# Conv-FFN with h normed into a second buffer, and adaLN sections moved from TensorE to VectorE

## The chip, the cores and the metric

The kernel runs on one core of one Trainium2 chip. The metric is the time of one execution on the device, in microseconds; the median of several runs is given.

## The reference, cut to what matters

Four layers over 384 tokens (128 context tokens, 256 latent tokens) of width 1024, all in fp32. Layer i uses mixer i mod 3 (gMLP, pooling, attention), so layers 0 and 3 are gMLP. Each mixer and each FFN has a pre-norm with its own scale and shift (adaLN), which differ for the two groups of tokens:

```
sh1, sc1, gt1, sh2, sc2, gt2 = split(silu(cond) @ w_ada[i] + b_ada[i], 6)
h = rms_norm(x, g_mix[i]) * (1 + sc1) + sh1
x = x + gt1 * mixer(h)
h = rms_norm(x, g_ffn[i]) * (1 + sc2) + sh2
x = x + gt2 * conv_ffn(h)

def conv_ffn(h, w_in, conv_w, conv_b, w_out):          # D_FF = 2816
    a, u = split(h @ w_in, 2)
    a = ap[:-2] * conv_w[0] + ap[1:-1] * conv_w[1] + ap[2:] * conv_w[2] + conv_b
    return (gelu(a) * u) @ w_out
```

## The kernel before

Activations lie transposed: features on the 128 partitions (KD = 8 tiles), tokens along the row. A product in fp32 accuracy is three fp32r matmuls: each weight chunk is split into whi (ScalarE, line 338) and wlo (VectorE, line 345), each activation into a high and a low part (hh, hl; gh, gl), and `mm3` (line 638) issues hi x hi, lo x hi, hi x lo.

Weights come as chunks of 128 x 1024 through one SP queue into a ring of five raw buffers (`load`, `free`); split chunks have four buffers. `w_get` takes the next chunk and has the three after it split; the split of a chunk waits until TensorE has finished the chunk four before it. The order of the instructions on every engine is that of the program. The chunks of w_ada for later layers are woven into the same list of chunks by the table `ADA` ("ad": line 380, two products with a running sum on VectorE per section of 128 rows; "ap": line 398, four matmuls per section on TensorE, 8 records in the profile). `EDGES` says how many weight chunks of a stage go by before its first section and after its last.

Before each FFN, `prep` (line 582 to 588) writes hh, hl = the two parts of x times A, not yet normed, and puts the shift into two more columns: rows of TE = 386 columns. So the input matmuls can start before the sum of squares is complete. `ffn` (line 641) runs f = 0 and 1 together (chunks "fr"), takes the sums of squares (`stats`, line 521) at k = stat_k, builds a diagonal R from the reciprocal roots, spreads it with a matmul over all partitions and copies it to rbs (line 697). Then f = 2 to 21 follow, two chunks and 48 matmuls each. The epilogue of a tile (`epi_a`, `epi_b`, `epi_c`) multiplies a and u with rbs on VectorE (lines 657, 661), adds the shift's column (be, line 671), does the convolution (lines 673 on ScalarE, 675 on VectorE), Gelu (681), gg = (u + bu) * gelu in two instructions (684, one per group of tokens; bu is read from PSUM), and splits gg into gh and gl. f's epilogue stands in the stage of f + 1; those of 0 and 1 both in f = 2. Matmul outputs have six PSUM banks in turn: four for f = 0 and 1, two for each later f. Then `out_proj` multiplies gh, gl with w_out; its residuals feed the next `prep`.

Of the kernel before, what the change touches and what calls it, by code (L numbers as in the profile page):

```python
# [34 lines left out]
TE = T + 2  # L35
BUFS = 5
# [21 lines left out]
EDGES = {(0, "gv"): (2, 1), (0, "go"): (5, 0), (3, "gv"): (5, 2), "fi": (0, 6), (3, "go"): (5, 2)}  # L58
# [212 lines left out]
class Prog:  # L271
    def __init__(self, ctx, tc, a):
# [5 lines left out]
        self.wsp = pool("wsp", 4)  # L278
        self.tmp = pool("tmp", 2)
# [235 lines left out]
    def stats(self, *parts):  # L515
# [1065 lines left out]
```

## Time and profile before

| | |
|---|---|
| median of 3 runs | 1789.53 us (1789.23 to 1791.93) |
| profiled execution | 1789.65 us, span of its instructions 1787.8 us |
| busy in the span | TensorE 1766.3 us (matmuls overlap), VectorE 1387.9, ScalarE 873.9 |
| adaLN sections | 136 on VectorE (272 products), 40 on TensorE (320 records) |

The span runs from the first to the last instruction of the program; the execution's own time has a little more around it. Busy time of TensorE is modelled, since matmuls are pipelined: the distance from matmul to matmul says more. A releaser ("<-") is the engine whose event ended a wait.

### The profile page before, as it was taken

The numbers are of one execution on the slowest core, as the hardware profiler recorded it, in microseconds if no ns is written. First come the engines' busy times: TensorE is split into PE (matmuls) and PEld (weight loads), VectorE is DVE, ScalarE is ACT, GpSimd is POOL, SyncE is SP. The second block draws the span as 40 slices with busy tenths as digits, with TensorE's granted clock in tenths as the row PEclk, the third lists the DMA queues.
The fourth block names the chain that finished last, engine by engine and source line by source line (L and its number), as shares of the span: only waits on it lengthen the run. The fifth ranks groups of instructions, "written<-read, shape, count | busy, mean of one in ns | idle before, by whom it ended". The sixth has DMA issues, their size and how long they took to land.

```text
span 1787.8 us, 26990 instructions
## 1 busy us (share of the span) xinstructions
PE 1766.3 (99%) x10326; PEld 1682.8 (94%) x10326; DVE 1387.9 (78%) x2456; ACT 873.9 (49%) x1556; POOL 1.8 (0%) x30
## 2 busy tenths in 40 slices
PE   7999999999999999999999999999999999999999
PEld 5799899999998999999778999999988999999999
DVE  5877689998876888797787788878775787888732
ACT  3634335555445555432568465553354443555531
POOL 0000000000000000000000000000000000000000
PEclk9999999999999999999999999999999999999999
DMA  9775565554653444466543444436645255444341
GB/s 328 283 238 179 211 218 176 177 176 168 208 201 122 146 163 175 148 234 228 177 148 131 139 156 159 165 118 214 204 170 196 96 175 177 142 153 143 123 150 57
DMA packets 87637, 311.65 MB, mean 174 GB/s; under 512 B 10450, under 2 KB 10962, under 8 KB 87252
## 3 DMA queue, kind: packets, MB, share of 16 engines
q1 hardware_dynamic: 87364, 309.92, 49.8%
q8 instruction: 81, 1.33, 0.3%
q14 instruction: 48, 0.39, 0.1%
q10 hardware_dynamic: 144, 0.01, 0.0%
HBM read 308.06 MB, written 1.84 MB: 173 GB/s over the span
## 4 chain that ended last, share of the span: by engine, by line
PE 84%; DVE 10%; ACT 3%; issue 2%; DMA 1%; SPq 0%; DVEq 0%; ACTq 0%
PE mm L638 65%; PE mm L762 6%; DVE junk L380 3%; DVE wlo L345 2%; ACT whi L338 1%; PE S L638 1%; PE mm L806 1%; DMA wraw<-wts 1%; DVE ct L675 1%; PE S L1035 1%; PE psa L398 1%; PE adaT L638 1%; PE mm L928 1%; PE psa L762 1%; PE adaT L762 1%
## 5 line engine op out<-in xcount | busy, mean ns | idle before, releaser
L345 DVE TENSOR_TENSOR wlo<-wraw,whi 128x1024 fp32r<-128x1024 f32 (+2 forms) x390 | 465.8, 1200 | 188.7 <-ACT whi L338 187.7
L338 ACT ACTIVATE whi<-wraw 128x1024 fp32r<-128x1024 f32 (+2 forms) x390 | 399.7, 1035 | 305.3 <-PE mm L638 189.1
L638 PE MATMUL mm<-hh,whi 128*128 128x386 f32 (+1 forms) x1664 | 426.6, 341 | 0.0
L638 PE MATMUL mm<-hh,wlo 128*128 128x386 f32 (+1 forms) x1664 | 423.9, 340 | 0.7 <-DVE wlo L345 0.2
L638 PE MATMUL mm<-hl,whi 128*128 128x386 f32 (+1 forms) x1664 | 421.3, 338 | 0.0
L380 DVE SCALAR_TENSOR_TENSOR junk<-wraw,condb 128x1024 bf16<-128x1024 f32 x272 | 332.2, 1221 | 7.6 <-ACT condb L1499 2.7
L638 PEld LDWEIGHTS mm<-hh,whi 128*128 128x128 f32 x1664 | 300.6, 188 | 4.8 <-issue 2.1
L638 PEld LDWEIGHTS mm<-hh,wlo 128*128 128x128 f32 x1664 | 303.1, 188 | 2.0 <-DVE wlo L345 1.9
L638 PEld LDWEIGHTS mm<-hl,whi 128*128 128x128 f32 x1664 | 303.3, 188 | 0.0
L638 PE MATMUL mm<-gh,wlo 128*128 128x384 f32 x704 | 193.6, 336 | 0.0
L638 PE MATMUL mm<-gl,whi 128*128 128x384 f32 x704 | 193.6, 336 | 0.0
L638 PE MATMUL mm<-gh,whi 128*128 128x384 f32 x704 | 193.6, 336 | 0.0
L681 ACT ACTIVATE ct<-ct 128x385 f32<-128x385 f32 x88 | 46.1, 527 | 178.2 <-DVE ct L675 178.1
L638 PEld LDWEIGHTS mm<-gl,whi 128*128 128x128 f32 x704 | 128.5, 188 | 0.0
L638 PEld LDWEIGHTS mm<-gh,wlo 128*128 128x128 f32 x704 | 128.5, 188 | 0.0
L638 PEld LDWEIGHTS mm<-gh,whi 128*128 128x128 f32 x704 | 128.4, 188 | 0.0
L675 DVE SCALAR_TENSOR_TENSOR ct<-ab,par,ct 128x385 f32<-128x385 f32 x176 | 109.1, 621 | 22.3 <-ACT ct L673 17.4
L684 DVE SCALAR_TENSOR_TENSOR gg<-u,mm,ct 128x128 f32<-128x128 f32 (+1 forms) x176 | 66.3, 419 | 49.1 <-ACT ct L681 49.1
L586 ACT ACTIVATE hh<-x,A 128x128 fp32r<-128x128 f32 x96 | 43.2, 457 | 104.9 <-DVE x L453 94.1
L671 ACT ACTIVATE ab<-a,be 128x128 f32<-128x128 f32 (+1 forms) x176 | 70.7, 450 | 2.6
L657 DVE TENSOR_TENSOR a<-mm,rbs 128x384 f32<-128x384 f32 x88 | 48.6, 552 | 20.5 <-PE mm L638 14.5
L673 ACT ACTIVATE ct<-ab,par 128x385 f32<-128x385 f32 x88 | 62.7, 712 | 3.4
(301 smaller groups left out, 1961.9 us busy)
## 6 DMA issues: line engine op xcount, KB each, us to landing
wraw<-wts SPq DMA_DIRECT2D x562, 512.0 KB, 3.3
wraw<-wts SPq DMA_DIRECT2D x12, 256.0 KB, 2.6
wraw<-wts SPq DMA_DIRECT2D x8, 384.0 KB, 4.1
x<-x SPq DMA_DIRECT2D x4, 384.0 KB, 4.3
mx<-mix SPq DMA_DIRECT2D x1, 1280.0 KB, 7.1
y<-x SPq DMA_DIRECT2D x3, 384.0 KB, 3.1
condb<-condb SPq DMA_DIRECT2D x1, 1024.0 KB, 8.6
ws<-a_w_s SPq DMA_DIRECT2D x2, 512.0 KB, 4.0
```

The lines of the kernel that those rows point to most:

```text
L338: nc.scalar.activation(hi[:, :n], t[:, :n], AF.Copy)
L345: nc.vector.tensor_tensor(out=lo[:, :n], in0=t[:, :n], in1=hi[:, :n].bitcast(F32), op=ALU.subtract)
L380: nc.vector.scalar_tensor_tensor(out=self.junk.bitcast(BF16), in0=w, scalar=1.0, in1=self.condb[:, c, :], op0=ALU.mult, op1=ALU.mult, accu ...
L586: nc.scalar.activation(self.hh[:, d, t0:t1], self.x[:, d, t0:t1], AF.Copy, scale=A[:, d, c:c + 1])
L638: nc.tensor.matmul(o, w[:, c:c + nw], r, start=(first and p == 0), stop=(last and p == 2))
L657: nc.vector.tensor_tensor(out=a1, in0=pa[:, 0:T], in1=rbs, op=ALU.mult)
L671: nc.scalar.activation(ab[:, p0:p1], a1[:, t0:t1], AF.Identity, bias=be[:, c:c + 1])
L673: nc.scalar.activation(t, ab[:, 1:T + 2], AF.Identity, scale=cw[1], bias=cb)
L675: nc.vector.scalar_tensor_tensor(out=t, in0=ab[:, i:i + T + 1], scalar=cw[i], in1=t, op0=ALU.mult, op1=ALU.add)
L681: nc.scalar.activation(t, t, GELU)
L684: nc.vector.scalar_tensor_tensor(out=g[:, t0:t1], in0=u1[:, t0:t1], scalar=bu[:, c:c + 1], in1=t[:, t0 + c:t1 + c], op0=ALU.add, op1=ALU.mult)
L762: nc.tensor.matmul(ps[n][i], hs, w[p == 1][:, c:c + 512], start=(k == 0 and p == 0), stop=(k == 7 and p == 2))
```

## The change

There are two buffers hb[0] and hb[1] where hh and hl were one. For f = 0, 1 and 2 (NR = 3) an FFN works as before. Meanwhile `put_act` norms x again with rbs into the other buffer, with shift, in plain rows of 384: one multiply on VectorE, two affine activations and a copy on ScalarE, one subtract on VectorE for each of the eight k. From f = 3 on the matmuls read this buffer and 384 columns, and the epilogue has no multiply with rbs, copies a from PSUM, and has Gelu in two parts and one product. The epilogue of f = 0 stands in f = 2, that of 1 in f = 3, and so on; in f = 8 two are done, from then on the distance is one tile again. stat_k is 3 in place of 5 (layer 1: 6 in place of 7), and the spread comes two k after the sums, where the stage has that many left. The products of f = 14 to 21 are stored over the first buffer, which is no longer read. The gMLP's second half, the attention's qS and layer 3's u products use the buffers in the same way. 24 sections move from "ap" to "ad", (0,3), (0,4) and others change stage, and an FFN's sections lie between its 8th and its 40th chunk.

```
 ADA = {
-    (0, "gv"): [("ad", 0, 2)],
-    (0, "gu"): [("ad", 0, 3), ("ap", 0, 4)],
-    (0, "go"): [("ad", 0, 5), ("ap", 1, 1)],
-    (0, "fi"): [("ad", 1, 2), ("ad", 1, 0), ("ad", 1, 4, 0, 3)],
-    (0, "fo"): [("ad", 1, 4, 3, 8), ("ad", 1, 3)],
-    (1, "fi"): [("ad", 1, 5), ("ad", 2, 1, 0, 5)],
-    (1, "fo"): [("ad", 2, 1, 5, 8), ("ad", 2, 0), ("ad", 2, 4)],
-    (2, "nm"): [("ap", 2, 3, 0, 6)],
-    (2, "qkv"): [("ap", 2, 3, 6, 8)],
-    (2, "at"): [("ap", 2, 2), ("ap", 2, 5)],
-    (2, "fi"): [("ad", 3, 1), ("ad", 3, 2, 0, 3)],
-    (2, "fo"): [("ad", 3, 0), ("ad", 3, 2, 3, 8)],
-    (3, "gv"): [("ad", 3, 4), ("ad", 3, 3, 0, 1)],
-    (3, "go"): [("ad", 3, 3, 1, 8)],
+    (0, "gv"): [("ad", 0, 4)],
+    (0, "gu"): [("ad", 0, 2), ("ad", 0, 3, 0, 2)],
+    (0, "go"): [("ad", 0, 3, 2, 8), ("ad", 0, 5, 0, 3)],
+    (0, "fi"): [("ad", 0, 5, 3, 8), ("ad", 1, 1), ("ad", 1, 2), ("ad", 1, 0, 0, 5)],
+    (0, "fo"): [("ad", 1, 0, 5, 8), ("ad", 1, 4), ("ad", 1, 3)],
+    (1, "fi"): [("ad", 1, 5), ("ad", 2, 1), ("ad", 2, 0)],
+    (1, "fo"): [("ad", 2, 4), ("ad", 2, 3)],
+    (2, "nm"): [("ap", 2, 2, 0, 6)],
+    (2, "qkv"): [("ap", 2, 2, 6, 8)],
+    (2, "at"): [("ap", 2, 5)],
+    (2, "fi"): [("ad", 3, 1), ("ad", 3, 2)],
+    (2, "fo"): [("ad", 3, 0), ("ad", 3, 4, 0, 4)],
+    (3, "gv"): [("ad", 3, 4, 4, 8), ("ad", 3, 3, 0, 4)],
+    (3, "go"): [("ad", 3, 3, 4, 8)],
     (3, "fi"): [("ad", 3, 5)],
 }
-EDGES = {(0, "gv"): (2, 1), (0, "go"): (5, 0), (3, "gv"): (5, 2), "fi": (0, 6), (3, "go"): (5, 2)}
+EDGES = {(0, "gv"): (2, 1), (0, "go"): (5, 0), (3, "gv"): (5, 2), "fi": (8, 4), (3, "go"): (5, 2)}
...
+    def put_act(self, k, A, rbs, hi, lo, sh):
+        nc = self.nc
+        t = self.tmp.tile([128, T], F32, tag="sq", name="nt")
+        nc.vector.tensor_tensor(out=t, in0=self.x[:, k, :], in1=rbs, op=ALU.mult)
+        for c, (t0, t1) in enumerate(GRPS):
+            nc.scalar.activation(t[:, t0:t1], t[:, t0:t1], AF.Identity, scale=A[:, k, c:c + 1], bias=sh[:, k, c:c + 1])
+        nc.scalar.activation(hi[:, k, :], t, AF.Copy)
+        return lambda: nc.vector.tensor_tensor(out=lo[:, k, :], in0=t, in1=hi[:, k, :].bitcast(F32), op=ALU.subtract)
...
+    def plain(self, n):
+        w, o = KD * T, PLAIN[n]
+        return [self.hb[n][:, w * i + o:w * i + w + o].rearrange("p (k t) -> p k t", t=T) for i in range(2)]
...
     def ffn(self, l, pr, follow, stat_k):
...
+        nh, nl = self.plain(1 - self.cur)
+        tail = self.plain(self.cur)
...
+            gh, gl = ([own[i][:, f, :] if f < NG else tail[i][:, f - NG, :] for f in range(NF)] for i in range(2))
...
             def epi_a(f, pa, pu):
+                if f >= NR:
+                    return f, pa, None, pu, None
...
-                    nc.scalar.activation(ab[:, p0:p1], a1[:, t0:t1], AF.Identity, bias=be[:, c:c + 1])
+                    if f < NR:
+                        nc.scalar.activation(ab[:, p0:p1], a1[:, t0:t1], AF.Identity, bias=be[:, c:c + 1])
+                    else:
+                        nc.scalar.activation(ab[:, p0:p1], a1[:, t0:t1], AF.Copy)
...
+                if f >= NR:
+                    for c, (t0, t1) in enumerate(GRPS):
+                        nc.scalar.activation(g[:, t0:t1], t[:, t0 + c:t1 + c], GELU)
+                    nc.vector.tensor_tensor(out=g, in0=u, in1=g, op=ALU.mult)
+                    return g
...
+            def norm(n):
+                ks, to_norm[:] = to_norm[:n], to_norm[n:]
+                for i in range(0, len(ks), 2):
+                    for lo in [self.put_act(k, pr["A"], rbs, nh, nl, sh) for k in ks[i:i + 2]]:
+                        lo()
...
                     if k == stat_k:
                         R = self.diag(self.stats(pr["acc"], pr["sq"]))
+                    if k == stat_k + 2:
+                        nc.scalar.activation(rbs, self.spread(R), AF.Copy)
+                        R = None
                     self.mm3([(b[i], 512 * k2 + 128 * i) for i in range(4)], w, (hh[:, k, :], hl[:, k, :]),
                              k == 0, k == 7)
-            nc.scalar.activation(rbs, self.spread(R), AF.Copy)
+                    if k > stat_k + 1:
+                        norm(2)
+            if R is not None:
+                nc.scalar.activation(rbs, self.spread(R), AF.Copy)
+            norm(2)
             prev = [(0, b[0], b[1]), (1, b[2], b[3])]
             for f in range(2, NF):
-                pa, pu = self.bank()[:, :TE], self.bank()[:, :TE]
+                w0 = TE if f < NR else T
+                pa, pu = self.bank()[:, :w0], self.bank()[:, :w0]
+                now, prev = (prev, []) if f == 8 else (prev[:1], prev[1:])
...
+                    if f < NR:
+                        norm(3)
                     for k4 in range(4):
                         k = 4 * kk + k4
-                        self.mm3([(pa, 256 * k4), (pu, 256 * k4 + 128)], w, (hh[:, k, :], hl[:, k, :]), k == 0, k == 7)
-                prev = [(f, pa, pu)]
+                        r = (hh[:, k, :], hl[:, k, :]) if f < NR else (nh[:, k, :], nl[:, k, :])
+                        self.mm3([(pa, 256 * k4), (pu, 256 * k4 + 128)], w, r, k == 0, k == 7)
+                prev.append((f, pa, pu))
...
-            pr = self.ffn(l, pr, follow, 7 if kind == 1 else 5)
+            pr = self.ffn(l, pr, follow, 6 if kind == 1 else 3)
```

## Rows read from the trace of the kernel before

**Rows 1.** The page's busy list: busy us, share, instructions.

```profile
PE 1766.3 (99%) x10326; PEld 1682.8 (94%) x10326; DVE 1387.9 (78%) x2456; ACT 873.9 (49%) x1556; POOL 1.8 (0%) x30
```

**Rows 2.** The chain that ended last, shares by line, whole span.

```profile
by line: PE mm L638 65.2%; PE mm L762 6.4%; DVE junk L380 3.0%; DVE wlo L345 2.4%; issue 1.9%; ACT whi L338 1.4%; PE S L638 1.4%; PE mm L806 1.2%; DMA wraw<-wts 1.2%; DVE ct L675 1.1%; PE S L1035 1.0%; PE psa L398 0.7%; PE adaT L638 0.7%; P
```

**Rows 3.** Stretches: us, then busy of PE, PEld, DVE, ACT, POOL; clock; DMA.

```profile
272.00:443.50 171.50, 170.83 (x960) 169.43 (x960) 154.17 (x251) 92.72 (x165) 0.00 (x0) 1.00 0.50 173
443.50:536.00 92.50, 92.50 (x538) 92.50 (x537) 76.52 (x130) 43.24 (x71) 0.00 (x0) 1.00 0.59 201
584.00:753.70 169.70, 169.70 (x961) 169.70 (x960) 146.22 (x235) 95.08 (x168) 0.00 (x0) 1.00 0.45 159
```

**Rows 4.** Waits of TensorE and its weight loads, 60 us to the end: total, times, longest.

```profile
PE Tps L421 <- ACT T L1244: 1.0, 1, 1.0
...
PEld mm L638 <- DVE wlo L345: 1.9, 4, 0.5
```

**Rows 5.** Matmuls in two stretches (xcount), and a piece of the chain.

```profile
600.00:740.00 140.00, 140.00 (x793) 1.00 0.47 166
770.00:830.00 60.00, 60.00 (x348) 1.00 0.77 261
...
163.23 8.44 PE mm L638 x48
```

**Rows 6.** Groups by line: busy us and mean ns; line 398.

```profile
L398 PE MATMUL psa<-wraw,cond 128*32 128x256 f32 x320 | 24.3, 389 | 0.8 <-DMA wraw<-wts 0.8
```

**Rows 7.** Pieces of the chain, layers 1 and 2: start, us, what.

```profile
583.97 261.38 PE mm L638 x1488
...
1009.19 10.59 PE mm L638 x60
1019.78 1.23 PE cs L521 x12
...
1028.12 265.57 PE mm L638 x1512
```

**Rows 8.** Timeline of VectorE, layer 2: start, us, what.

```profile
1022.28 0.56 DVE L530 TENSOR_TENSOR R<-ident,rs 128x384 f32<-128x384 f32 x1
```

**Rows 9.** Timeline of ScalarE, layer 2.

```profile
1028.16 0.49 ACT L697 ACTIVATE rbs<-adaT 128x384 f32<-128x384 f32 x1 [3.77 <-PE adaT L536]
...
1030.27 0.79 ACT L671 ACTIVATE ab<-a,be 128x128 f32<-128x128 f32 x2
...
1033.38 1.28 ACT L681 ACT_TABLE_LOAD   x1
```

**Rows 10.** Timeline of VectorE, layer 0, one tile f.

```profile
394.19 1.22 DVE L380 SCALAR_TENSOR_TENSOR junk<-wraw,condb 128x1024 bf16<-128x1024 f32 x1
...
396.60 1.27 DVE L675 SCALAR_TENSOR_TENSOR ct<-ab,par,ct 128x385 f32<-128x385 f32 x2
398.46 0.76 DVE L684 SCALAR_TENSOR_TENSOR gg<-u,mm,ct 128x128 f32<-128x128 f32 x2 [0.59 <-ACT ct L681]
399.41 1.23 DVE L345 TENSOR_TENSOR wlo<-wraw,whi 128x1024 fp32r<-128x1024 f32 x1 [0.19 <-ACT whi L338]
400.56 0.55 DVE L568 TENSOR_TENSOR gl<-gg,gh 128x384 fp32r<-128x384 f32 x1
401.02 0.55 DVE L657 TENSOR_TENSOR a<-mm,rbs 128x384 f32<-128x384 f32 x1
...
401.96 1.21 DVE L345 TENSOR_TENSOR wlo<-wraw,whi 128x1024 fp32r<-128x1024 f32 x1
403.09 1.22 DVE L380 SCALAR_TENSOR_TENSOR junk<-wraw,condb 128x1024 bf16<-128x1024 f32 x1
```

**Rows 11.** Timeline of ScalarE, layer 0, the same tile.

```profile
397.91 0.53 ACT L681 ACTIVATE ct<-ct 128x385 f32<-128x385 f32 x1 [3.44 <-DVE ct L675]
398.34 1.04 ACT L338 ACTIVATE whi<-wraw 128x1024 fp32r<-128x1024 f32 x1
399.29 0.51 ACT L567 ACTIVATE gh<-gg 128x384 fp32r<-128x384 f32 x1
```

More of the change, by code (lines that the diff above doesn't have):

```diff
@@ L475, in sqrt_table @@
         nc = self.nc
-        d = self.tmp.tile([128, 1], F32, tag="dmy", name="dmy")
+        d = self.tmp.tile([128, 1], F32, tag="dmy", name="dmy", bufs=1)
         nc.scalar.activation(d, self.ones[:, 0:1], AF.Sqrt)
@@ L628, in prep_squares, with use @@
         return res, after
+    def use(self, n):
+        self.cur = n
+        w = KD * TE
+        self.hh, self.hl = (self.hb[n][:, w * i:w * i + w].rearrange("p (k t) -> p k t", t=TE) for i in range(2))
+    def plain(self, n):
+        w, o = KD * T, PLAIN[n]
+        return [self.hb[n][:, w * i + o:w * i + w + o].rearrange("p (k t) -> p k t", t=T) for i in range(2)]
     def mm3(self, outs, whl, rhl, first, last, nw=128):
@@ L703, in ffn @@
                         sts = []
-                        w = self.w_get("fi", mid=lambda: sts.extend([epi_a(*p) for p in prev]))
+                        w = self.w_get("fi", mid=lambda: sts.extend([epi_a(*p) for p in now]))
                         ts = [epi_b(st) for st in sts]
@@ L745, in gmlp @@
         nc = self.nc
-        hh, hl = self.hh[:, :, 0:T], self.hl[:, :, 0:T]
-        te = T if pr is None else TE
+        hb = self.cur if pr is None else 1 - self.cur
+        vh, vl = self.plain(hb)
+        tail = self.plain(1 - hb)
         with self.tc.tile_pool(name=f"gmlp{l}", bufs=1) as gp:
             v = gp.tile([128, 3, DG], F32, tag="v", name="v")
-            ga = gp.tile([128, 16, T], F32R, tag="ga", name="ga")
-            gb = gp.tile([128, 16, T], F32R, tag="gb", name="gb")
+            own = [gp.tile([128, 8, T], F32R, tag=n, name=n) for n in ("ga", "gb")]
+            ga, gb = ([own[i][:, c, :] if c < 8 else tail[i][:, c - 8, :] for c in range(16)] for i in range(2))
             ws = gp.tile([128, 8, 128], F32, tag="ws", name="ws")
@@ L869, in gmlp @@
             for m in range(m0, 8):
-                b = [self.bank()[:, :te] for _ in range(2)]
+                b = [self.bank()[:, :T] for _ in range(2)]
                 for kk in range(2):
@@ L1268, in store_lo @@
                                         op=ALU.subtract)
-            nc.scalar.activation(self.tmp.tile([128, 1], F32, tag="dmy", name="dmy"), self.ones[:, 0:1], AF.Exp)
+            nc.scalar.activation(self.tmp.tile([128, 1], F32, tag="dmy", name="dmy", bufs=1), self.ones[:, 0:1], AF.Exp)
             put(2)
@@ L1390, in attention @@
             store_lo(NP - 2)
-            self.out_proj("o", oh[:, :, 0, :], oh[:, :, 1, :], 8, l, 2, after, banks, drain, 0)
+            self.out_proj("o", [oh[:, s, 0, :] for s in range(NP)], [oh[:, s, 1, :] for s in range(NP)], 8, l, 2, after,
+                          banks, drain, 0)
             ex.close()
@@ L1400, in run @@
         self.x = self.const.tile([128, KD, T], F32, name="x")
-        self.hh = self.const.tile([128, KD, TE], F32R, name="hh")
-        self.hl = self.const.tile([128, KD, TE], F32R, name="hl")
-        self.par = self.const.tile([128, NPAR], F32, name="par")
+        self.hb = [self.const.tile([128, 2 * KD * TE], F32R, name=f"hb{i}") for i in range(2)]
+        self.use(0)
+        self.par = self.const2.tile([128, NPAR], F32, name="par")
         self.cst = self.const.tile([128, NCST], F32, name="cst")
@@ L1461, in a0_put @@
         def a0_put(d, A):
-            self.put([d], lambda k: A, rbs, self.hh[:, :, 0:T], self.hl[:, :, 0:T], 0)
+            self.put([d], lambda k: A, rbs, *self.plain(0), 0)
         nc.scalar.activation(self.cond[:, :, 0:2], cin, AF.Silu)
```

55 lines of the change are left out of this document (33 added, 22 removed).

## The prediction

> **What bounds the kernel now.** I read the page's busy list first, then the chain that ended last, then stretches of single stages, then timelines. TensorE is busy 99% of the span [rows 1], but matmuls are pipelined, so this says little; the chain says more: most of it is matmuls, 65% line 638 alone, with VectorE's adaLN products (junk), weight splits (wlo) and convolution (ct) as the next links [rows 2]. The stretches show where VectorE is near the limit: 154.17 of 171.50 us in the input stage of layer 0's FFN, 146.22 of 169.70 in layer 1's, 76.52 of 92.50 in layer 0's output stage, all at clock 1.00 [rows 3]. After the first 60 us TensorE hardly waits: the longest single wait of a matmul is 1.0 us, and VectorE's weight splits hold back the weight loads of line 638 four times, 1.9 us together [rows 4]. So the kernel is bound by matmul time, with VectorE close behind in layers 0 and 1. What takes matmul time away is worth its time; what makes VectorE or ScalarE later shows soon.
>
> **What is taken from TensorE.** (1) Columns. Tiles f = 3 to 21 of each FFN read 384 columns instead of 386: 19 tiles x 48 matmuls x 4 layers = 3648. Less the two records that straddle a stretch's edges, 140 us hold 791 matmuls of 386 columns, 177.0 ns each, and 60 us hold 346 of 384, 173.4 ns [rows 5]. 3648 x 3.6 ns = 13.1 us. Layer 3's gMLP changes 288 in the same way: 1.0 us. Layer 0's gMLP has 384 columns already, in rows of 386: 48 matmuls in 8.44 us, 175.8 ns [rows 5]. So most of the 3.6 ns goes with the rows' place, not with two columns; stored 384 apart, 384 x 2.4 ns = 0.9 us more. The bound below: if the new rows lie no better, only the 1.2 ns of the two columns, 4.7 us in place of 15.0.
> The Trainium skill (TensorE: Matmul & The Clock Gate, section "Back-to-back issue gap") gives an isolated warm matmul N/2.4 ns plus a fixed 2.5. Two columns would be 0.83 ns by that, 3936 matmuls 3.3 us, and the sum below some 11 us worse; the rows are longer than its figure at both widths and differ by more.
> (2) 24 adaLN sections leave TensorE. A section is 8 matmul records, 320 for 40 sections, 24.3 us [rows 6], 0.61 us each. The 16 in layer 0 stand in a stage that TensorE sets: 9.8 us. Layer 2's eight fill an attention stage with gaps. The chain holds 0.7% of 1787.8, 12.5 us, of psa [rows 2]; less the 9.8, 2.7 us are left for 24 attention sections, so eight give 0.9 (bounds 0 and 4.9).
> (3) The 1.9 us of waits in layer 0's FFN [rows 4] go, if VectorE is no longer late; it will be, below, and the new sum replaces them.
> Together 13.1 + 1.0 + 0.9 + 9.8 + 0.9 + 1.9 = 27.6 us.
>
> **What is put on the way: the norm before f = 3.** Layer 2 as the model, by its own clock. The input stage starts at 1009.19; 60 matmuls (five k) take 10.59, 2.12 per k; the twelve sums of squares take 1.23; f = 2 starts at 1028.12 [rows 7]. In the change the sums come at k = 3 and end at 1016.8. R was ready 1.8 us after their end (1022.84 against 1021.01) [rows 7, 8], so the spread at k = 5, at 1021.0, has it. Before, the spread followed three k after 1021.0, at 1027.4, and the copy rbs started at 1028.16 and took 0.49 [rows 9]: it ends 1.2 us after the spread begins, now at 1022.2. TensorE has three k and f = 2 left, so f = 3 is due at 1036.5 as before (1028.12 + 8.47).
> f = 3 takes the banks of f = 0: there are six, four for f = 0 and 1, two for f = 2. They are free only after f = 0's product gg, which reads its bias from the bank. All eight norms now stand before that epilogue in the order of both ScalarE and VectorE. One pair: VectorE multiply 0.55 (as gl) [rows 10]; ScalarE two affine parts 0.79 (as ab) [rows 9], 0.1 to the dependent copy, copy 0.51 [rows 11], the second k 1.31 later; VectorE subtract. With 0.03 per hand-over that is 0.55 + 0.03 + 2.72 + 0.03 + 0.46 = 3.8 us, and the next pair can't start sooner, since VectorE's subtract of the second k stands ahead of it. Four pairs 15.2, plus 1.6 for a weight split between the first two: norms end at 1039.0. Then f = 0: multiply 0.55, be 0.2, ab 0.8 and 0.1, ct 0.71 (1041.4), VectorE's two ct 1.28, in the shadow of which the table load of 1.28 runs [rows 9], Gelu 0.55, gg 0.76: 1044.1. **f = 3 waits 7.6 us**, in layers 0, 2 and 3. Bound below: ScalarE alone, without any wait (8 x 1.31, two splits, the epilogue, table load, Gelu, gg), ends at 1039.4: 2.9 us. I take the chain, for the two engines hand over twice in every pair.
> Queued behind this wait are all later matmuls, and ScalarE's splits of the chunks whose buffers they free; VectorE and ScalarE catch up meanwhile. In layers 0 and 2 the first adaLN section (after the split of chunk 9) comes ahead of f = 1's epilogue, now one tile later than before: 0.6 us at f = 4 in layer 2.
> Layer 1 spreads after the stage. f = 2 starts at 583.97 [rows 7], rbs ends at 584.5, one pair to 588.3; f = 0's multiplies and a weight split 2.1, ct 1.6; then three more norms (3.8 + 2.5) before its Gelu: table load 1.28, Gelu, gg, 600.4 against 592.4 due: 8.0. Three norms, a split and an adaLN section (2.41) then stand before f = 1's gg, 615.7 against 608.8: 6.9 more.
> Sum: 3 x 7.6 + 0.6 + 14.9 = 38.3 us; bound below 3 x 2.9 + 4.4 = 13.1.
>
> **VectorE per tile, with more adaLN.** In layer 0 VectorE sets the pace already: 403.09 - 394.19 = 8.90 us per tile with one section [rows 10], against 48 x 177.0 = 8.50 of TensorE. A section is 396.60 - 394.19 = 2.41. The new epilogue drops a and u (0.93) and halves gg to one instruction (0.46). But VectorE's wait for Gelu stays, since nothing stands between ct and gg, and Gelu is two activations now, 0.8 as ab instead of 0.53. The next weight split waits for whi, which starts 0.1 before Gelu's end and takes 1.04 [rows 11]: from ct's end to wlo's start were 1.54 us (397.87 to 399.41), with gg inside; 0.27 for the longer Gelu makes it 1.80. Per tile: ct 1.27 + 1.80 + wlo 1.15 + gl 0.46 + wlo 1.13 = 5.81, plus 2.41 per section. The sections of a stage now lie in 32 of its 44 chunks, 16 tiles: layer 0 has 26 (1.625 per tile), 9.73 us; layer 1 24 (1.5), 9.43; layer 2 16, 8.22; layer 3 8, 7.02; against 48 x 173.4 = 8.32 of TensorE. Layers 2 and 3 fit. Layer 0 loses 1.41 x 16 = 22.6, layer 1 1.11 x 16 = 17.8, less the lead that VectorE can lose first: before, 18 tiles of 0.40 too much are 7.2 us, of which TensorE felt 1.9, so 5.3. **17.3 and 12.5 us.** Bound below: with before's idle of 0.78 per tile (0.59 and 0.19, [rows 10]) in place of 1.34, 0.85 and 0.55 too much, 8.3 and 3.5.
> Layer 0's output stage takes six more sections, 76.52 + 6 x 2.5 = 91.5 of 92.50 us [rows 3]: bounds 0 and 5, I take 1. Its other stages have room.
>
> **Costed at nothing.** Weight chunks are as many and as large, in another order on the one SP queue; a section no longer held for TensorE frees its ring buffer as VectorE finishes it. Products of f = 14 to 21 over the first buffer, qS and the gMLP's tail in it: the old readers are matmuls long done. Single buffers for ms and dmy: each is used once per stage. The multiplies gone from layer 3's gMLP lighten an idle VectorE. If VectorE were at its limit there, four fewer sections there still leave it room.
>
> **Sum.** 1789.65 (the profiled execution; span 1787.83 plus 1.8 around it; the median of runs is 1789.53) - 27.6 + 38.3 + 17.3 + 12.5 + 1.0 = 1831.2. I say 1831.
>
> **Rivals.**
> A. Slower, as above, 1809 to 1852, half way to the bounds below, and as far above: 0.60.
> B. The norms are done in time: f = 0's gg ends before f = 3 is due, and sections fit between. Place: the first 15 us after rbs in each FFN. It decides if the norms take under 9 us in place of 16.8. For it: VectorE and ScalarE are idle much of the input stage's first 18 us, and the sums come two k earlier. Against: ScalarE's own work alone is over that. 1789.65 - 27.6 = 1762. 0.13.
> C. The bank wait is real but the sections fit, because Gelu's wait is filled: 1789.65 - 27.6 + 38.3 + 1 = 1801. Against it: 8.90 before, with the wait in it. 0.10.
> D. After a wait of this length the clock falls. Every stretch shown has 1.00, but with no wait over 1.0 us behind it [rows 3, 4], so the trace shows neither. If the tile after each of five long waits ran at half the clock, 5 x 8.3 = 42 us more, 1872; a part of it is likelier, 1850 to 1860. 0.12. The Trainium skill (TensorE: Matmul & The Clock Gate, section "HAM oscillation — how this bites in real kernels") says that long waits between bursts of matmuls bring the slow clock back each time; no run here shows it yet.
> E. All costs at their lower bounds: 1789.65 - 27.6 + 13.1 + 11.8 = 1787.0, about no change; 0.05.
>
> **Numbers.** 0.2% is 3.6 us, about what a measurement of this kernel can tell from no change. Faster: B and a little of E, 0.15. Same: 0.04. Slower: A, C, D, 0.81. The range 1787 to 1852 holds A, C, part of D and the edge of E; B lies outside. A's own range is 1809 to 1852.
>
> **What will show it.** f = 3 of each FFN: a wait of TensorE on gg of 7 to 8 us, two such waits in layer 1, and VectorE's row of norms ending some 17 us after rbs. Input stages of layers 0 and 1 some 15 to 25 us longer, with steady waits on VectorE (wlo or gg); layers 2 and 3 4 to 6 us longer. Line 638 at 173.4 ns with 384 columns; 128 records of psa left at line 398's successor. It is wrong if VectorE or ScalarE keep another order than the program's, if f = 3's banks are others than f = 0's, or if the Gelu wait vanishes.

## The result, and the profile after

The changed kernel takes 1845.65 us (median, 1842.43 to 1846.58), the kernel before 1789.74 beside it: 1.031 times as long, with a 95% interval of 1.0295 to 1.0321. The prediction was 1831, with 1787 to 1852 as its range. The span of the profiled execution is 1843.5 us, 55.7 more than before.

The table has the distance from the first matmul of a stage to the first of the next (line 638 before, 669 after, in the timelines), and what the terms of the prediction make of each stage: for the input stages the waits, the sections and 19 x 48 matmuls x 3.6 ns = 3.3 us of columns, in layer 0 less the 1.9 us of waits that it had before.

| stage | before | after | measured | predicted |
|---|---|---|---|---|
| layer 0, gMLP u and output | 157.6 | 144.5 | -13.1 | -10.7 |
| layer 0, FFN input | 191.0 | 213.0 | +22.1 | +19.7 |
| layer 0, FFN output and pooling | 121.0 | 126.4 | +5.5 | +1.0 |
| layer 1, FFN input | 189.0 | 215.0 | +26.1 | +24.1 |
| layer 1, FFN output; attention | 255.4 | 253.7 | -1.7 | -0.9 |
| layer 2, FFN input | 188.8 | 195.8 | +7.0 | +4.9 |
| layer 3, gMLP | 214.4 | 214.7 | +0.4 | -1.0 |
| layer 3, FFN input | 188.8 | 197.2 | +8.4 | +4.3 |
| the rest | | | +1.0 | 0 |

The page after: busy list, the chain by engine and line, and the group of the adaLN sections left on TensorE.

```profile
PE 1762.9 (96%) x10128; PEld 1683.5 (91%) x10128; DVE 1383.0 (75%) x2364; ACT 884.9 (48%) x1637; POOL 1.8 (0%) x30
...
PE 68%; DVE 19%; ACT 9%; issue 3%; DMA 1%; DVEq 0%; ACTq 0%
PE mm L669 51%; DVE junk L389 6%; PE mm L834 6%; DVE wlo L354 5%; DVE ct L716 3%; ACT whi L347 2%; ACT nt L580 2%; PE S L669 1%; PE mm L878 1%; ACT hb L581 1%; ACT gg L725 1%; DVE gl L587 1%; PE adaT L669 1%; PE S L1109 1%; DMA wraw<-wts 1%
...
L407 PE MATMUL psa<-wraw,cond 128*32 128x256 f32 x128 | 9.0, 386 | 0.1
```

TensorE and VectorE do a little less work than before [rows 1], yet the matmuls of `mm3` have gone from 65.2% of the chain [rows 2] to 51%, and the sections, the weight splits and the new norm's lines stand in it. TensorE now waits, as this list for the span from 60 us on says (total, times, longest):

```profile
PE mm L669 <- DVE gg L730: 27.0, 7, 8.7
PE mm L669 <- ACT be L697: 13.1, 3, 4.4
PE mm L669 <- ACT whi L347: 7.2, 6, 2.5
PE mm L669 <- DVE wlo L354: 5.1, 8, 0.8
PE mm L669 <- DVE gg L726: 4.8, 3, 1.9
```

Before, the longest was 1.0 us [rows 4]. The stretches after (us; busy of PE, PEld, DVE, ACT, POOL; granted clock; DMA): the input and output stage of layer 0's FFN and the input stage of layer 1's, as in [rows 3], then a steady stretch of layer 2 and the time behind the waits at f = 3 of layers 2 and 3.

```profile
260.00:453.70 193.70, 175.72 (x960) 171.53 (x959) 165.44 (x254) 94.64 (x184) 0.00 (x0) 0.96 0.54 182
453.70:551.00 97.30, 93.94 (x533) 93.36 (x532) 86.95 (x145) 41.15 (x69) 0.00 (x0) 0.98 0.64 215
600.00:795.00 195.00, 175.67 (x956) 172.56 (x955) 163.01 (x250) 97.40 (x190) 0.00 (x0) 0.94 0.52 172
...
1110.00:1190.00 80.00, 80.00 (x464) 80.00 (x463) 69.03 (x100) 43.18 (x86) 0.00 (x0) 1.00 0.57 190
...
1086.00:1096.00 10.00, 10.00 (x54) 10.00 (x53) 9.06 (x15) 5.19 (x9) 0.00 (x0) 0.89 0.45 159
1588.00:1600.00 12.00, 12.00 (x56) 12.00 (x55) 8.17 (x14) 5.86 (x11) 0.00 (x0) 0.77 0.39 132
```

In the first three TensorE has 18, 3 and 19 us without work; in each stretch of [rows 3] it had under 1. The columns came as predicted: less the two records that straddle the edges, 80 us hold 462 matmuls, 173.2 ns each, against 177.0 [rows 5].

The wait itself, on TensorE in layer 2: the end of f = 2 and the start of f = 3.

```profile
1076.02 0.52 PE L669 MATMUL mm<-hb,whi 128*128 128x386 f32 x2
1080.92 0.45 PE L669 MATMUL mm<-hb,whi 128*128 128x384 f32 x1 [4.38 <-ACT be L697]
1085.39 0.66 PE L669 MATMUL mm<-hb,whi 128*128 128x384 f32 x1 [4.03 <-DVE gg L730]
...
1086.49 1.49 PE L669 MATMUL mm<-hb,whi 128*128 128x384 f32 x4
...
1090.43 0.86 PE L669 MATMUL mm<-hb,whi 128*128 128x384 f32 x4
```

The bank of a is free once f = 0's multiply and bias have read it, that of u once gg has: 4.38 + 4.03 = 8.4 us. Between the two waits one matmul runs, in 0.45 us. Behind them four matmuls take 1.49 us in place of 0.86: the lower of the two clock levels, 1.2 GHz. In VectorE's row for the same time, the last two pairs of norms and f = 0's epilogue:

```profile
1071.97 1.02 DVE L578 TENSOR_TENSOR nt<-x,rbs 128x384 f32<-128x384 f32 x2
1074.14 0.56 DVE L582 TENSOR_TENSOR hb<-nt,hb 128x384 fp32r<-128x384 f32 x1 [1.15 <-ACT hb L581]
1075.57 0.56 DVE L582 TENSOR_TENSOR hb<-nt,hb 128x384 fp32r<-128x384 f32 x1 [0.88 <-ACT hb L581]
1076.05 1.02 DVE L578 TENSOR_TENSOR nt<-x,rbs 128x384 f32<-128x384 f32 x2
1078.20 0.56 DVE L582 TENSOR_TENSOR hb<-nt,hb 128x384 fp32r<-128x384 f32 x1 [1.14 <-ACT hb L581]
1079.63 0.56 DVE L582 TENSOR_TENSOR hb<-nt,hb 128x384 fp32r<-128x384 f32 x1 [0.87 <-ACT hb L581]
1080.11 0.55 DVE L695 TENSOR_TENSOR a<-mm,rbs 128x384 f32<-128x384 f32 x1
...
1084.49 0.76 DVE L730 SCALAR_TENSOR_TENSOR gg<-u,mm,ct 128x128 f32<-128x128 f32 x2 [0.59 <-ACT ct L728]
```

And ScalarE's:

```profile
1061.67 0.49 ACT L752 ACTIVATE rbs<-adaT 128x384 f32<-128x384 f32 x1 [1.67 <-PE adaT L545]
...
1072.56 0.99 ACT L580 ACTIVATE nt<-nt,prm,A 128x128 f32<-128x128 f32 x2 [1.09 <-DVE nt L578]
1073.58 0.53 ACT L581 ACTIVATE hb<-nt 128x384 fp32r<-128x384 f32 x1
1074.01 0.97 ACT L580 ACTIVATE nt<-nt,prm,A 128x128 f32<-128x128 f32 x2
```

VectorE multiplies, waits 1.15 and 0.88 us for ScalarE, subtracts; then ScalarE waits 1.09 us for the next multiply. A pair takes 1076.05 - 1071.97 = 4.08 us, the whole row 1080.19 - 1062.16 = 18.0 us from the end of rbs. Both engines are idle by turns, while TensorE waits.

### The profile page after: what moved, and what is told of

The parts are those of the page before. It is cut to its first block, busy times and chain, and to the rows that moved or that the text cites. A ratio compares the mean times of both kernels' runs of the same rounds, so it can differ in the third digit from the quotient of the medians.

```text
span 1843.5 us, 26653 instructions
## 1 busy us (share of the span) xinstructions
PE 1762.9 (96%) x10128; PEld 1683.5 (91%) x10128; DVE 1383.0 (75%) x2364; ACT 884.9 (48%) x1637; POOL 1.8 (0%) x30
## 4 chain that ended last, share of the span: by engine, by line
PE 68%; DVE 19%; ACT 9%; issue 3%; DMA 1%; DVEq 0%; ACTq 0%
PE mm L669 51%; DVE junk L389 6%; PE mm L834 6%; DVE wlo L354 5%; DVE ct L716 3%; ACT whi L347 2%; ACT nt L580 2%; PE S L669 1%; PE mm L878 1%; ACT hb L581 1%; ACT gg L725 1%; DVE gl L587 1%; PE adaT L669 1%; PE S L1109 1%; DMA wraw<-wts 1%
## 5 line engine op out<-in xcount | busy, mean ns | idle before, releaser
L669 PE MATMUL mm<-hb,whi 128*128 128x384 f32 (+1 forms) x4064 | 902.3, 341 | 49.7 <-DVE gg L730 27.0
L669 PEld LDWEIGHTS mm<-hb,whi 128*128 128x128 f32 x4064 | 731.9, 191 | 57.2 <-issue 28.4
L669 PE MATMUL mm<-hb,wlo 128*128 128x384 f32 (+1 forms) x2032 | 527.1, 340 | 4.4 <-DVE wlo L354 4.3
L389 DVE SCALAR_TENSOR_TENSOR junk<-wraw,condb 128x1024 bf16<-128x1024 f32 x320 | 391.0, 1222 | 8.4 <-ACT condb L1574 2.7
L669 PEld LDWEIGHTS mm<-hb,wlo 128*128 128x128 f32 x2032 | 373.4, 191 | 6.9 <-DVE wlo L354 6.9
L669 PE MATMUL mm<-gh,whi 128*128 128x384 f32 x448 | 124.1, 338 | 2.5 <-ACT whi L347 2.5
L669 PE MATMUL mm<-gh,wlo 128*128 128x384 f32 x448 | 124.0, 338 | 0.8 <-DVE wlo L354 0.8
L669 PE MATMUL mm<-gl,whi 128*128 128x384 f32 x448 | 123.8, 337 | 0.0
L834 PE MATMUL mm<-whi,hb 128*128 128x512 f32 x320 | 87.5, 399 | 0.0
L726 DVE TENSOR_TENSOR gg<-mm,gg 128x384 f32<-128x384 f32 x76 | 42.4, 558 | 47.4 <-ACT gg L725 46.7
L834 PEld LDWEIGHTS mm<-whi,hb 128*128 128x128 f32 x320 | 60.6, 190 | 15.9 <-ACT rb L1560 0.8
```

The lines of the kernel that those rows point to most:

```text
L389: nc.vector.scalar_tensor_tensor(out=self.junk.bitcast(BF16), in0=w, scalar=1.0, in1=self.condb[:, c, :], op0=ALU.mult, op1=ALU.mult, accu ...
L669: nc.tensor.matmul(o, w[:, c:c + nw], r, start=(first and p == 0), stop=(last and p == 2))
L726: nc.vector.tensor_tensor(out=g, in0=u, in1=g, op=ALU.mult)
L834: nc.tensor.matmul(ps[n][i], hs, w[p == 1][:, c:c + 512], start=(k == 0 and p == 0), stop=(k == 7 and p == 2))
```

## The experiments

The table has the medians, and the ratio to the kernel before beside them (1789.2 to 1790.3 in the three groups of runs) with its 95% interval.

| run | what | us | ratio |
|---|---|---|---|
| half_norm | four norms in place of eight | 1809.03 | 1.0102 [1.0086, 1.0117] |
| lead3 | multiplies up to four k ahead | 1835.16 | 1.0257 [1.0243, 1.0271] |
| norm_late | norms in f = 3 to 6 | 1864.81 | 1.0424 [1.0406, 1.0441] |
| keep_warm | matmuls to fill the waits | 1840.72 | 1.0284 [1.0268, 1.0299] |
| ada_back | norms alone, sections as before | 1834.05 | 1.0246 [1.0231, 1.0261] |
| ada_only | sections alone, FFN as before | 1837.61 | 1.027 [1.0255, 1.0286] |
| pitch386 | plain rows 386 apart | 1853.64 | 1.0355 [1.0341, 1.0369] |
| moved | no norms, eight sections moved | 1793.19 | 1.0017 [1.0008, 1.0026] |
| fit | the same, norms fitted in layers 2, 3 | 1788.72 | 0.999 [0.9981, 0.9999] |
| fit2 | fit, 8 sections in place of 11 | 1787.78 | 0.9992 [0.9983, 1.0001] |
| fit3 | fit2, 13 and 19 sections | 1784.98 | 0.9977 [0.9968, 0.9987] |

**half_norm: is the wait the norms' chain?**

```
-            to_norm = list(range(KD))
+            to_norm = list(range(KD // 2))
...
-                        r = (hh[:, k, :], hl[:, k, :]) if f < NR else (nh[:, k, :], nl[:, k, :])
+                        r = (hh[:, k, :], hl[:, k, :]) if f < NR else (nh[:, k % 4, :], nl[:, k % 4, :])
```

> The changed kernel with only the first four of the eight norm steps per FFN; tiles f = 3 to 21 read the normed k = 0 to 3 twice (this part of the computation is left wrong). Theory (the two waits at f = 3 are the length of the chain of norm pairs, 4.08 us per pair): two pairs less end the chain 8.2 us sooner, so the 8.05 us at f = 3 fall to under 0.5 in layers 0, 2 and 3; layer 2's input stage goes from 195.8 to about 187.8 us, layer 3's from 197.2 to 189, layer 0's by 8; layer 1's first wait falls from 8.6 to about 6.4 and its second from 5.2 to under 1, about 7 us. Sum 31, so 1815 us (1806 to 1822, the lower end if the slow clock behind the waits goes as well). Rival (the waits belong to the turn of the PSUM banks or to the longer way of f = 0's epilogue, whatever the norms take): the same waits, 1843 to 1846.

1809.03. In layers 0, 2 and 3 the two waits at f = 3, 8.2 to 8.4 us together, are now one of 0.5; layer 1's 8.7 and 5.3 us are 6.0 and 1.8. Layer 2's input stage takes 187.6 us, its f = 2 8.49 in place of 13.04; layer 0's is 9.7 shorter, layer 1's and layer 3's 10.9 each, more than expected. In layer 3, where f = 4 takes 8.32 us with the wait and without, the clock's loss goes too (mean granted clock of the whole run 0.993 in place of 0.983); in layers 0 and 1 VectorE and ScalarE also have less to do, and no run takes these two apart. So the wait goes with the length of the row of norms, as the theory said. Layer 0's output stage got 2.8 us longer, though nothing in it was changed; lead3 shows the same (3.3), and why stays open.

**lead3: work or hand-overs?**

```
+                for k in ks:
+                    if len(los) == 4:
+                        los.pop(0)()
+                    t = fp.tile([128, T], F32, tag="nt", name="nt", bufs=4)
+                    los.append(self.put_act(k, pr["A"], rbs, nh, nl, sh, t))
+                while los and not to_norm:
+                    los.pop(0)()
```

> The changed kernel with four buffers for the norms' intermediate in place of two: VectorE's multiplies may run up to four k ahead of its subtracts. Theory (the wait at f = 3 is the length of the chain in which the two engines hand over twice per pair, 4.08 us): ScalarE's part, 1.5 to 1.6 us per k, now follows without gaps, eight norms take about 13.9 us in place of 16.3, and the 8.05 us of waits at f = 3 fall by 2.4 in layers 0, 2 and 3; in layer 1 two to three less. 1846 - 10 = 1836 us (1832 to 1840). Rival (the sum of the work of VectorE and ScalarE sets the wait, however it is interleaved, as with the norms moved behind f = 2): no change, 1844 to 1848.

1835.16, the sum that the theory had. Its list of TensorE's waits, the two lines that answer to those above:

```profile
PE mm L668 <- DVE gg L729: 26.5, 7, 7.2
...
PE mm L668 <- ACT be L696: 5.9, 3, 2.0
```

The wait on be fell from 4.4 to 2.0 in each of three layers, f = 2 of layers 0, 2 and 3 from 13.04 to 10.63. In ScalarE's timeline of layer 2 the six norms behind the split stand without a gap, 1.44 us each:

```profile
1062.80 0.99 ACT L579 ACTIVATE nt<-nt,prm,A 128x128 f32<-128x128 f32 x2 [1.76 <-DVE nt L577]
...
1070.00 0.97 ACT L579 ACTIVATE nt<-nt,prm,A 128x128 f32<-128x128 f32 x2
```

(1070.00 - 1062.80) / 5 = 1.44 us. So some 2.4 us of the 8.4 are hand-overs. Of the rest 2.0 us are ScalarE's row, which still ends after the due time, and 4.0 the wait on gg: f = 0's own epilogue, which follows the norms. gg's total hardly fell, since it holds layer 1's two waits and the second wait of the others, which starts when the first ends. That the sum came out is in part luck: the input stages of layers 0, 1 and 3 fell by 3.7 to 4.0 us, layer 2's by 1.3 only (its f = 3 rose from 14.02 to 15.11), and layer 0's output stage rose by 3.3.

**norm_late: would a later place do?** NR = 7, both first epilogues in f = 2, no norm before f = 3, one per chunk in f = 3 to 6.

```
-NR = 3
+NR = 7
...
-                    if f < NR:
-                        norm(3)
+                    if 2 < f < NR:
+                        norm(1)
```

> The changed kernel with the norms moved behind the epilogues of f = 0 and 1: both epilogues stand in f = 2 as before the change, the eight norms come one per chunk in f = 3 to 6, and the first normed tile is f = 7. Theory: the waits at f = 3 (and f = 4 in layer 1) go, and with them the low clock behind them; layers 2 and 3 come to 186 to 189 us per input stage (195.8 and 197.2 now); layers 0 and 1 stay late by VectorE's work and gain 4 to 10 us each: 1815, between 1805 and 1825. Rival (the wait at f = 3 comes from something else than the norms' place, such as the buffer's old readers or weights): f = 3 or f = 7 still waits 8 us, and the time stays within 5 us of 1845.65.

1864.81, 50 more than expected, and slower than the change itself: my expectation was wrong. Layer 3's f = 7, the first normed tile, takes 18.45 us. VectorE's timeline in its f = 3, with the first two norms:

```profile
1598.05 0.55 DVE L695 TENSOR_TENSOR a<-mm,rbs 128x384 f32<-128x384 f32 x1
...
1601.62 0.55 DVE L578 TENSOR_TENSOR nt<-x,rbs 128x384 f32<-128x384 f32 x1
1603.78 0.56 DVE L582 TENSOR_TENSOR hb<-nt,hb 128x384 fp32r<-128x384 f32 x1 [1.61 <-ACT hb L581]
...
1606.75 0.55 DVE L578 TENSOR_TENSOR nt<-x,rbs 128x384 f32<-128x384 f32 x1
1608.92 0.56 DVE L582 TENSOR_TENSOR hb<-nt,hb 128x384 fp32r<-128x384 f32 x1 [1.61 <-ACT hb L581]
1609.40 0.55 DVE L695 TENSOR_TENSOR a<-mm,rbs 128x384 f32<-128x384 f32 x1
```

A norm put as a unit (multiply, wait 1.61, subtract) costs VectorE 1604.25 - 1601.62 = 2.63 us, of which 1.0 is work. Two in a tile make it 1609.40 - 1598.05 = 11.35 us, without a section, against 8.5 of TensorE. The lag adds up over four tiles, and TensorE pays it at f = 7: 4 x 2.85 = 11.4 us by these rows, 18.45 - 8.32 = 10.1 measured. What costs is the wait inside each norm, in tiles that leave no room for it. With one whole norm in a tile the same rows give about 11.35 - 2.63 = 8.7 us, an estimate; no run has that.

**keep_warm: what is the clock's part?** Dummy matmuls into the spare bank fill the wait before f = 3 (46; layer 1 48, and 28 before f = 4).

```
+                fill = {3: 48 if l == 1 else 46, 4: 28 if l == 1 else 0}.get(f, 0)
+                if fill:
+                    dps = self.ps_bank()[:, :T]
+                    for i in range(fill):
+                        nc.tensor.matmul(dps, hh[:, 7, 0:128], hh[:, 7, 0:T], start=(i == 0), stop=(i == fill - 1))
```

> The changed kernel with 46 matmuls of 384 columns (8.0 us) into a free bank ahead of f = 3's first matmul in each FFN, in layer 1 48, and 28 more ahead of f = 4; their result is not read. They fill the waits and no more. Theory with the clock: about 100 of the 128 matmuls that now start some 340 ns apart in place of 173 run at the full clock, 100 x 0.17 = 17 us, of which VectorE's lateness in layers 0 and 1 takes some back: 1833, between 1827 and 1839. Rival (VectorE and ScalarE set the pace behind the waits, so a slow clock costs nothing there): 1845 or a little more.

1840.72, the mean granted clock 0.996. The gain is 4.9 us, under half of what was expected. In layer 3 the tiles f = 2 to 5 take 13.04 + 15.44 + 8.32 + 8.32 = 45.1 us after, 16.59 + 9.17 + 8.32 + 8.32 = 42.4 with the fill; in layer 2, 43.7 and 43.65, since there f = 4 and 5 now take 8.99 and 8.90: TensorE at full clock waits for VectorE's gg, 0.60 us in f = 3 and 0.41 in f = 4, for VectorE is behind as well. There, and in layer 0, the slow clock passes in the shadow of an engine that is late anyway.

**ada_back and ada_only: one part each.** The first has before's tables in the changed kernel, the second the new tables in the kernel before:

```
 (0, "fi"): [("ad", 1, 2), ("ad", 1, 0), ("ad", 1, 4, 0, 3)]                       # before
 (0, "fi"): [("ad", 0, 5, 3, 8), ("ad", 1, 1), ("ad", 1, 2), ("ad", 1, 0, 0, 5)]   # after
 "fi": (0, 6)     # before
 "fi": (8, 4)     # after
```

> The changed kernel with the section tables ADA and EDGES of the kernel before: 40 sections on TensorE again, 19 and 13 on VectorE in the input stages of layers 0 and 1 instead of 26 and 24. Theory (the norms cost their waits, and the extra sections cost VectorE's pace in layers 0 and 1): psa comes back, 10.7 us; 17.3 + 12.5 us of VectorE's lateness and part of the clock's share go; one section may fall between the norms in each of three layers, 2.4 us each: about 1818, between 1808 and 1828. Rival (only the waits at f = 3 and the clock behind them matter, the sections fit): the sections' way back to TensorE costs 10 us: about 1855.

> The kernel before with the new section tables ADA and EDGES alone, no second buffer. Theory: with the old epilogue a tile needs 6.49 us of VectorE plus 2.41 per section, 10.41 in layer 0 and 10.11 in layer 1 against 8.50 of TensorE; 16 tiles, less a lead of 5.3 us: 25 + 20 us lost, 10.7 gained: about 1825, between 1812 and 1838. Rival (VectorE has room for 24 more sections; the new place in the stage is harmless): 1789.7 - 10.7 = 1779.

1834.05 and 1837.61. The sections alone cost 48 us, and the rest of the change (norms, less what the columns gain) 44, together 56. The second run shows where sections go when VectorE has no room: layer 0's input stage +22.9, its output stage and pooling +12.2, layer 1's input +19.6 and output +3.6, layer 2's output +1.3, the input stages of layers 2 and 3 +0.1; the first gMLP stages, relieved of 16 sections on TensorE, give back 12.8. ada_back missed by 16, and that is the clock's share in its expectation: 1845.65 + 10.7 - 17.3 - 12.5 + 3 x 2.4 is 1834 without it, and 1818 takes 16 us more. The granted clock was still 0.986, and keep_warm prices all of the clock at 4.9. With a lead of 0 the sections stand between the norms, as expected: f = 2 and 3 of layer 0 take 14.9 and 16.2 us in place of 13.0 and 15.2. From f = 4 on a tile of layer 0 takes 8.32. That the parts do not add up I put down to the new epilogue, which is shorter on VectorE (5.81 us per tile in the prediction's sum, against 8.90 - 2.41 = 6.49 before [rows 10]); no run takes that apart.

**pitch386: columns or place?**

```
-        w, o = KD * T, PLAIN[n]
-        return [self.hb[n][:, w * i + o:w * i + w + o].rearrange("p (k t) -> p k t", t=T) for i in range(2)]
+        w = KD * TE
+        return [self.hb[n][:, w * i:w * i + w].rearrange("p (k t) -> p k t", t=TE)[:, :, 0:T] for i in range(2)]
```

> The changed kernel with the plain rows 386 apart in place of 384 (still 384 columns read). Theory (of the 3.6 ns per matmul, 2.4 go with the place of the rows and 1.2 with the two columns): a tile f that TensorE sets takes 48 x 175.8 = 8.44 us in place of 8.32, some 17 tiles in layers 2 and 3 each, 8 in layer 1, 4 in layer 0, and the two gMLPs' u products 0.9 and 0.7: about 7 us more, 1852 (1849 to 1855). Rival (two columns fewer give all of it): 8.32 per tile, 1844 to 1847.

1853.64, 8.0 us more for the same columns; but 3.1 of that are in layer 0's output stage, and it is the tiles that show the effect cleanly. A steady stretch of its layer 2:

```profile
1100.00:1190.00 90.00, 90.00 (x513) 90.00 (x512) 76.91 (x114) 45.51 (x89) 0.00 (x0) 1.00 0.58 187
```

Less the two at the edges 511 matmuls, 176.1 ns each; a tile takes 8.45 us, and 8.32 with the rows 384 apart. So of the 3.8 ns that a matmul gained, 2.9 are the rows' place. The isolated gap of the Trainium skill (TensorE: Matmul & The Clock Gate, section "Back-to-back issue gap") holds the width alone; by it this run would have changed nothing, and the measurement decides.

**moved, fit, fit2, fit3: what can be kept?** moved has no norms; only (0,4) leaves TensorE, and the gMLPs keep the plain rows. The others norm in layers 2 and 3 alone: two pairs at k = 5 and 6, then one k per tile, cut in three and spread over a tile:

```
+NRS = [22, 22, 7, 7]
...
                         ts = [epi_b(st) for st in sts]
+                        if f > 2:
+                            norm_dve()     # subtract of the k before, multiply of the next
...
+                        if f > 2:
+                            norm_act()     # affine parts and copy, behind the second split
...
-    (0, "go"): [("ad", 0, 5), ("ap", 1, 1)],                                      # before
+    (0, "gu"): [("ad", 0, 2), ("ad", 0, 3, 0, 5)],                                # fit3
+    (0, "go"): [("ad", 0, 3, 5, 8), ("ad", 0, 5, 0, 5), ("ap", 1, 1)],            # fit3
+    (0, "fi"): [("ad", 0, 5, 5, 8), ("ad", 1, 2), ("ad", 1, 0)],                  # fit3
+    (0, "fo"): [("ad", 1, 4), ("ad", 1, 3)],                                      # fit3
```

> No norms at all (all 22 tiles of each FFN as before the change), plain rows in both gMLPs, and of the 24 sections only the eight of (0,4) go to VectorE, put with their neighbours where VectorE has room: 8, 12 and 11 sections in layer 0's gMLP stages, 19 and 14 in its FFN. Theory (sections cost nothing where the stage leaves VectorE room, and TensorE gains 0.61 us for each): before 1789.7 - 4.9 (sections) - 0.9 - 1.0 (rows of the gMLPs) + 1 = 1784 us (1780 to 1788). Rival (any section more in layer 0 costs its 2.4 us, since VectorE sets the pace there): 8 x 2.4 - 6.8 more, 1802.

> As the kernel with no norms, but layers 2 and 3 norm h: two pairs at k = 5 and 6, while VectorE and ScalarE have room, then one k per tile in f = 3 to 6, VectorE's multiply where it waits for Gelu, ScalarE's part behind the second weight split and the subtract one tile later; tiles from f = 7 read the normed buffer, both first epilogues stand in f = 2 as before, sections start at chunk 12. Theory (the norms cost nothing where each engine has room and neither waits for the other): 15 tiles x 0.17 us = 2.6 us less in each of the two layers, waits of 1 each, 1784 - 3 = 1781 us (1776 to 1786). Rival (a norm adds its 2.6 us of alternating work wherever it stands): 8 x 2.6 less 3.6 of room per tile, 1790 to 1800.

> The fitted version with three sections less in layer 0's second gMLP stage (8 in place of 11, beside the eight that TensorE keeps), 20 in layer 0's FFN input stage (19), 16 in its output stage (14). Theory (the second gMLP stage was long because its sections stood in pairs ahead of the residuals): that stage goes from 80.7 to about 74.2 us, input stage +1, output stage +1: 1788.7 - 4.5 = 1784 us (1781 to 1787). Rival (layer 0's VectorE is full in every stage, so that sections cost 2.4 us wherever they go): 1788 to 1790.

> The same with 13 sections in the first gMLP stage (12) and 19 in the FFN input stage (20). Theory: the first gMLP stage has 8 us of VectorE's time free and takes it at nothing, the input stage gains 1: 1783 us (1780 to 1787). Rival (the first gMLP stage is at its limit): 2.4 us more than its sister.

moved (1793.19) missed by 9. Its first gMLP stage fell from 83.2 to 76.7 us, but the second, with 11 sections, rose from 74.4 to 80.3, though VectorE is busy only 60.95 of 77 us of it. It is full near the end:

```profile
225.00:235.00 10.00, 10.00 (x60) 9.96 (x59) 9.59 (x15) 2.13 (x2) 0.00 (x0) 1.00 0.70 218
235.00:245.00 10.00, 7.98 (x46) 7.66 (x44) 9.61 (x21) 3.12 (x7) 0.27 (x6) 1.00 0.75 257
```

There the stage's last two groups of 24 matmuls take 6.9 and 6.8 us in place of 4.2. The pairs of sections ahead of the residuals, which fit2's expectation blames, are not the cause: the kernel before and fit2 have two sections in a row there as well, and their stages take 74.4 and 74.9. fit2 has three sections less in the stage, so it is their number that counts. Another 1.8 us are the FFN input stages of layers 0 to 2, whose tiles take 8.52 us in place of 8.49 with the same 386 columns; the reason is open.

fit (1788.72) is 4.5 us below moved, with layers 2 and 3 at 187.4 and 186.4 us against 188.8 before; it is 8 us above its expectation because moved was 9 above. Its first two pairs are still whole and cost nothing, for f = 2 takes 8.49. With 8 sections the second gMLP stage took 74.9; but fit2 (4 above its expectation) lost that again in layer 0's input stage (197.0, f = 14 to 19 of 8.7 to 10.5 us). fit3 did not (190.0), and its first gMLP stage rose by the 2.4 us of the one section more. So fit3 came within its range by luck: the stage that was to take a section at nothing did not, and the input stage gained 7.0 us where 1 was expected. fit3, 1784.98, is 0.23% faster than the kernel before, its whole interval below 1. In its layer 2 the norm's multiply fills VectorE's wait for Gelu (0.59 us in [rows 10]), and the subtract of the k before finds its operand ready:

```profile
1050.15 1.28 DVE L719 SCALAR_TENSOR_TENSOR ct<-ab,par,ct 128x385 f32<-128x385 f32 x2 [0.41 <-ACT ct L717]
1051.34 0.55 DVE L763 TENSOR_TENSOR hb<-nt,hb 128x384 fp32r<-128x384 f32 x1
1051.81 0.55 DVE L754 TENSOR_TENSOR nt<-x,rbs 128x384 f32<-128x384 f32 x1
1052.28 0.75 DVE L733 SCALAR_TENSOR_TENSOR gg<-u,mm,ct 128x128 f32<-128x128 f32 x2
```

No wait stands in the last three rows. In norm_late the same norm had 1.61 us inside. TensorE's longest wait for it is 0.7 us.

## Why the prediction was right, and what it mis-sized

**The path.** Right: the kernel before was bound by matmul time with VectorE close behind, and the change gave its gain on TensorE away on the other two. Rival B (norms in time) fell with the waits, and C (sections fit) with the 16 us by which layer 0's tiles from f = 4 on are above 8.32, and which ada_back does not have.

**What TensorE saved.** The 3.6 ns per matmul were 3.8, and pitch386 shows the split the prediction made from rows of layer 0. Of line 398's successor 128 records are left, as expected. Layer 0's gMLP saved 13.1 in place of 10.7. Layer 3's gMLP was to give 1.0 and lost 0.4: its u stage fell by 0.7, two others rose by 0.5 each; why, no run tells.

**The wait at f = 3.** The mechanism, the place and the banks were right; one term was short. Due and epilogue came as computed: f = 3 was due 1076.37 - 1062.16 = 14.2 us after rbs (14.3 predicted) and f = 0's epilogue took 1085.25 - 1080.19 = 5.1 (5.1). The pair took 4.08, not 3.8, because the affine parts with scale and bias both from memory take 0.99 us; I had priced them as ab, 0.79 [rows 9]. Four pairs make 1.1 us more: 8.4 of wait, not 7.6. Layer 1's two were 8.7 and 5.3, predicted 8.0 and 6.9:

```profile
616.76 0.66 PE L669 MATMUL mm<-hb,whi 128*128 128x384 f32 x1 [8.68 <-DVE gg L730]
632.45 0.66 PE L669 MATMUL mm<-hb,whi 128*128 128x384 f32 x1 [5.33 <-DVE gg L730]
```

half_norm shows that the wait goes with the number of norms, and lead3 that 2.4 us of it are hand-overs between the two engines and not ScalarE's own work. All waits at f = 3 and 4 together are 38.9 us, 37.7 predicted.

**The clock**, rival D, was priced at nothing in the forecast and at 20 to 30 us as a rival. It does fall after each of these waits: 0.77 of full speed in the stretch behind layer 3's. By the Trainium skill (TensorE: Matmul & The Clock Gate, section "HAM oscillation — how this bites in real kernels") it should, and here the trace agrees. But it costs 4.9 us, by the medians of keep_warm; by its stages 2.7 in layer 3's input, 1.6 in layer 1's and nothing in those of layers 0 and 2, as VectorE holds those tiles anyway.

**VectorE per tile.** Right within 2%. One section's tile in layer 0 after, from ct to ct:

```profile
373.30 1.27 DVE L716 SCALAR_TENSOR_TENSOR ct<-ab,par,ct 128x385 f32<-128x385 f32 x2
375.26 0.56 DVE L726 TENSOR_TENSOR gg<-mm,gg 128x384 f32<-128x384 f32 x1 [0.69 <-ACT gg L725]
376.21 1.23 DVE L354 TENSOR_TENSOR wlo<-wraw,whi 128x1024 fp32r<-128x1024 f32 x1 [0.39 <-ACT whi L347]
...
381.37 1.27 DVE L716 SCALAR_TENSOR_TENSOR ct<-ab,par,ct 128x385 f32<-128x385 f32 x2
```

8.07 us with one section, 8.22 predicted; the wait for Gelu stayed, 0.69 + 0.39 us, as predicted (the two Gelu parts take 0.62, not 0.8). With 1.625 sections that is 9.6 per tile, above the 8.32 of TensorE.

**Layer 0's output stage** was the stage that was mis-sized most: 1 us, with bounds of 0 and 5; it lost 5.5. VectorE has 86.95 busy of 97.30 us there, and TensorE is without work for 3.4. ada_back and moved, with 13 and 14 sections there, take 120.9 and 121.0 us with pooling; fit3, with 16, 122.7; the change, with 19, 126.4. So the stage is full at 14 sections or so: in fit3 TensorE loses 1.2 of 91.6 us with VectorE busy 81.0. But the number of sections alone does not set the time: the same 19 make it 129.2 in half_norm and 133.1 in ada_only.

**What the sum was short of.** Of the 14.2 us the input stages are 10.6, the output stage 4.5, the gMLP of layer 3 1.4 and the start 1.0; the layer 0 gMLPs and the attention gave 3.2 back. In the input stages the waits are 1.2 of it. The five tiles right behind them take 12.7 us more than their waits and 8.32 each, where the prediction had nothing but 0.6 ("VectorE and ScalarE catch up meanwhile"). At full clock, in keep_warm, 4.3 of that come back; most of the rest stays, as waits for a VectorE that has not caught up. Against it the sections' terms were too large by 3.2 (16.0 and 10.6 us over 8.32 in layers 0 and 1, 17.3 and 12.5 predicted). So the total lies nearer to the forecast than its terms do.

## What to carry to other kernels

A piece of work that goes from one engine to another and back costs its whole length where the engines have no room for it, its waits included. Put each engine's part into a gap that the engine has anyway and take the result a step later: here the change without its sections lost 44 us in four layers, and fit gained 4.5 on moved in two. How much of that is the cutting and how much that fit puts one norm into a tile and not two, no run shows. Work may be moved to an engine that is idle on average only up to what single stages leave free; count per stage, waits included (stages were full here with VectorE 80 to 90% busy). And price an operation by a row with the same operands, not by one of the same shape.

## What the runs showed of the hardware

The same 384 columns take 173.2 ns per matmul from rows 384 apart and 176.1 from rows 386 apart. On ScalarE two parts of 128 and 256 columns take 0.53 us as a plain copy from PSUM (line 712), 0.80 with a bias from memory (line 710) and 0.99 with scale and bias (line 580). The granted clock fell to its lower level behind the waits (its mean was 0.77 in the 12 us behind layer 3's, of 8.3 us), and that cost 4.9 us beside the 40 of the two longest lines in the list of waits, since in layers 0 to 2 the engine that TensorE had waited for was still behind.
